# A sliding-window copy: some batches staged through SBUF beside a second ring of HBM-to-HBM copies

## The chip, the cores and the metric

The kernel runs on one core of a Trainium2 chip. The metric is the device time of one execution in microseconds. All runs here are of one core. The compute engines do next to nothing (0.2 us of 805.2 in the profile before): the program is DMA only, on the core's 16 DMA engines. Chips differ: on most of those used here the kernel before took 803 to 807 us, on one 818.8 us. Every kernel was therefore timed beside the kernel before on the same chip, and kernels from different chips are compared by that ratio.

## The reference

```python
batch, length, dim = (32, 4096, 256)       # x: float32, 134 MB
window_size, stride = 64, 32

n_windows = (length - window_size) // stride + 1      # 127
for i in range(n_windows):
    start = i * stride
    result[:, i] = x[:, start:start + window_size].copy()
```

Take 32 rows of 256 floats as one block: 32 KB. A batch has 128 blocks. Window i is block i followed by block i+1, 64 KB. So the output of a batch, 127 x 64 KB = 8.32 MB, is nearly twice its input of 4.19 MB. Each block except the first and the last goes to two places.

## The kernel before

It has several strategies. The one in use, `"d2d"`, copies windows straight from HBM to HBM on the one queue that the sync engine (SP) feeds. One DMA instruction copies 112 windows, a second one the remaining 15.

```python
STRATEGY = "d2d"
D2D_CHUNK = 112
D2D_NQ = 1

def _d2d_batch(q, x, out_flat, b, L, D, W, S, n_win):
    win_elems = W * D
    step_elems = S * D
    w0 = 0
    while w0 < n_win:
        nw = min(D2D_CHUNK, n_win - w0)
        src = bass.AP(x.tensor, x.offset + (b * L + w0 * S) * D,
                      [[step_elems, nw], [1, win_elems]])
        dst = out_flat[b * n_win + w0 : b * n_win + w0 + nw]
        q.dma_start(out=dst, in_=src, max_dma_last_dim=65536)
        w0 += nw

def _d2d(nc, x, out, B, L, D, W, S, n_win):
    out_flat = out.rearrange("b i w d -> (b i) (w d)")
    queues = [nc.sync, nc.scalar][:D2D_NQ]
    for b in range(B):
        _d2d_batch(queues[b % len(queues)], x, out_flat, b, L, D, W, S, n_win)
# ... (strategies "sbuf", "mix", "pair", "hybrid", which are not run)
```

Each window is one packet of 64 KB (4,064 in the trace, 32 x 127). Besides these, the trace has 992 small packets of 4 bytes, which is 32 x 16 + 32 x 15: as many as there are if every engine that takes part in a DMA posts one at its end, and if 112 windows run on 16 engines, seven each, and 15 windows on 15. I call them completion packets. From 739 us on, the shares of busy engines fit this too (0.94, or 15 of 16).

## Time and profile before

| | before |
|---|---|
| time | 807.23 us (806.14 to 807.51, 3 runs) |
| span of the profiled execution | 805.2 us |
| copied | 266.34 MB, so 266.34 MB read and 266.34 MB written |
| share of 16 engines' span with a packet | 98.3% |

These are lines of the profile page of the kernel before. The GB/s row has 40 equal slices of the span and counts each packet's bytes once. The queue's line gives packets, MB, and its packets' time as a share of 16 engines' span.

```profile
GB/s 313 355 322 332 342 316 352 322 339 335 319 358 313 322 352 319 348 329 335 339 316 358 319 329 348 313 361 319 335 335 332 342 322 339 332 322 332 326 335 254
q1 hardware_dynamic: 5056, 266.34, 98.3%
HBM read 266.34 MB, written 266.34 MB: 662 GB/s over the span
```

The engines always have a packet, but that does not say what limits the packets. The end of the run tells, because some engines run out of work there. This is the view by windows of time. Its columns are: window and its length, busy time of the one compute engine listed, clock, mean share of the 16 DMA engines that were busy, GB/s copied.

```profile
29.00:729.00 700.00, 0.00 (x0) 1.00 1.00 333
739.00:779.00 40.00, 0.00 (x0) 1.00 0.94 331
789.00:801.00 12.00, 0.00 (x0) 1.00 0.76 328
```

With 16, 15 and then 12 engines busy (shares 1.00, 0.94 and 0.76) the kernel copies 333, 331 and 328 GB/s. The packet records of the trace show the other side of it: a 64 KB packet takes 3.14 us on average with 16 engines busy and exactly 2.418 us with 12. An engine then does 65,536 B / 2.418 us = 27.1 GB/s, and at that rate 16 would do 434 (an estimate from the 2.418 us). Something that they share stops them at about 334 GB/s of copying, that is 668 GB/s of reads and writes.

### The profile page before, as it was taken

How to read it: one execution, taken by the hardware profiler on the slowest of the kernel's cores; microseconds unless marked ns; L12 is line 12 of the kernel's file. 1: busy time of each engine (PE TensorE's matmuls, PEld its weight loads, DVE VectorE, ACT ScalarE, POOL GpSimd, SP SyncE). 2: the span in 40 equal slices, each digit the busy share in tenths (PEclk: the TensorE clock that was granted, in tenths of full speed). 3: DMA queues.
4: the chain of work that ended last, by engine and by line, in shares of the span. 5: the costliest groups of instructions: out<-in, count | busy, mean ns of one | idle time of the engine just before them, and what ended most of it. 6: DMA issues, size and time to landing. Idle time of an engine off the chain costs nothing. (4 is left out here: it accounts for less than half of the span.)

```text
span 805.2 us, 109 instructions
## 1 busy us (share of the span) xinstructions
POOL 0.2 (0%) x4
## 2 busy tenths in 40 slices
POOL 0000000000000000000000000000000000000000
DMA  9999999999999999999999999999999999999995
GB/s 313 355 322 332 342 316 352 322 339 335 319 358 313 322 352 319 348 329 335 339 316 358 319 329 348 313 361 319 335 335 332 342 322 339 332 322 332 326 335 254
DMA packets 5056, 266.34 MB, mean 331 GB/s; under 512 B 992, under 2 KB 992, under 8 KB 992
## 3 DMA queue, kind: packets, MB, share of 16 engines
q1 hardware_dynamic: 5056, 266.34, 98.3%
HBM read 266.34 MB, written 266.34 MB: 662 GB/s over the span
## 5 line engine op out<-in xcount | busy, mean ns | idle before, releaser
L283 POOL MEMSET const-bfloat16-1.0<- 128x1 bf16 x1 | 0.1, 101 | 0.0
L283 POOL MEMSET const-uint8-127<- 128x1 uint8 x1 | 0.1, 101 | 0.0
L283 POOL MEMSET const-float32-0.0<- 128x1 f32 x1 | 0.1, 98 | 0.2 <-issue 0.2
L283 POOL MEMSET const-float32-1.0<- 128x1 f32 x1 | 0.1, 98 | 0.0
## 6 DMA issues: line engine op xcount, KB each, us to landing
out_dram<-in_x_dram SPq DMA_DIRECT2D x64, 100.5
```

The source lines that it names most:

```text
L283: nc = _bacc.Bacc("TRN2", target_bir_lowering=False, num_devices=1)
```

## The change

The intent: a batch that is staged in SBUF is read from HBM once instead of twice. Eight of the 32 batches (1, 5, ... 29) are loaded into SBUF tiles as [128 partitions x 32 KB] and stored twice, once as first halves of windows and once as second halves. The scalar engine (ACT) issues these on its own ring. The sync engine issues the other 24 batches as HBM-to-HBM copies on its ring, as before. To use 128 partitions, each store covers 128 half windows, one too many; the extra half lands in a window of a neighbouring batch, and that window is copied again after the store has landed. Windows that don't divide by 16 are cut otherwise: windows 113 to 125 of the 16 even batches go in one copy, meant to give each engine one batch, and other leftovers go in 4 KB pieces, 16 to a window. That each engine has one batch of that copy, and one piece of every window of the others, is an assumption.

The core of the diff, with cuts:

```diff
-STRATEGY = "d2d"
-def _d2d_batch(q, x, out_flat, b, L, D, W, S, n_win): ...
-# (all other strategies)
+class Copier:
+    def windows(self, q, b, w0, n):            # n windows of 64 KB
+        ... [[2 * blk, n], [1, 2 * blk]] <- [[blk, n], [1, 2 * blk]], max_dma_last_dim=65536
+    def windows_of(self, q, b0, step, n_b, w0, n):   # the same n windows of n_b batches
+        ...
+                out=self.oap((b0 * self.nw + w0) * 2 * blk,
+                    [[step * self.nw * 2 * blk, n_b], [2 * blk, n], [1, 2 * blk]]),
+                in_=self.xap(b0 * self.nb + w0,
+                    [[step * self.nb * blk, n_b], [blk, n], [1, 2 * blk]]),
+    def _shared(self, q, window, block, wstep, bstep, n, parts):   # 4 KB pieces, parts=16
+        e = 2 * blk // parts
+        ... [[e, parts], [wstep * 2 * blk, n], [1, e]] <- [[e, parts], [bstep * blk, n], [1, e]]
+    def load(self, q, t, b): ...      # 128 blocks of 32 KB -> 128 partitions
+    def store(self, q, t, b, half): ...
+class Staging: ...    # 4 tiles; semaphores loaded[i], stored[i]
...
+    with tc.tile_critical():
+        st.run(ring_s)
+
+        for b in sorted(evens + odds):
+            c.windows(ring_d, b, 1, 112)
+        c.windows_of(ring_d, 0, 2, 16, 113, last - 113)
+        for b in odds:
+            c.shared(ring_d, b, 113, n_win - 113)
+        c.shared_of(ring_d, odds[0], 4, len(odds), 0)
+        c.shared_of(ring_d, 0, 4, 8, 0)
+        c.shared_of(ring_d, 2, 4, 8, last)
+
+        for g in range(n_st - 1):
+            st.wait_stored(ring_d, g)
+        c.shared_of(ring_d, 0, 4, n_st - 1, last)
+        c.shared_of(ring_d, 2, 4, n_st - 1, 0)
+        st.wait_stored(ring_d, n_st - 1)
+        c.shared(ring_d, staged[-1] - 1, last, 1)
+        c.shared(ring_d, staged[-1] + 1, 0, 1)
+        ring_d.wait_ge(c.done, c.total)
```

More of the change, by code (lines that the diff above doesn't have):

```diff
@@ L4 @@
 import concourse.tile as tile
-from concourse import bass_utils, mybir
+from concourse import mybir
 from concourse._compat import with_exitstack
-STRATEGY = "d2d"
-NSB = 7
-D2D_CHUNK = 112
-def _d2d_batch(q, x, out_flat, b, L, D, W, S, n_win):
-    win_elems = W * D
-    step_elems = S * D
-    w0 = 0
-    while w0 < n_win:
-        nw = min(D2D_CHUNK, n_win - w0)
-        src = bass.AP(
-            x.tensor,
-            x.offset + (b * L + w0 * S) * D,
-            [[step_elems, nw], [1, win_elems]],
-        )
-        dst = out_flat[b * n_win + w0 : b * n_win + w0 + nw]
-        q.dma_start(out=dst, in_=src, max_dma_last_dim=65536)
-        w0 += nw
@@ L30 @@
-D2D_NQ = 1
-def _d2d(nc, x, out, B, L, D, W, S, n_win):
-    out_flat = out.rearrange("b i w d -> (b i) (w d)")
-    queues = [nc.sync, nc.scalar][:D2D_NQ]
-    for b in range(B):
-        _d2d_batch(queues[b % len(queues)], x, out_flat, b, L, D, W, S, n_win)
-class _SbufBatch:
-    def __init__(self, tc, ctx, x, out, B, L, D, W, S, n_win, bufs=3):
-        assert W % S == 0 and L % S == 0
-        self.m = W // S
-        self.n_blocks = L // S
-        assert self.n_blocks <= 128
-        self.blk = S * D
-        self.n_win = n_win
-        self.x_blocks = x.rearrange("b (n s) d -> b n (s d)", n=self.n_blocks)
-        self.out_rows = out.rearrange("b i w d -> b i (w d)")
-        self.pool = ctx.enter_context(tc.tile_pool(name="swin_sbuf", bufs=bufs))
-        self.dtype = x.dtype
-        self.chunks = []
-        w0 = 0
-        for cnt in (64, 48, 16, 15):
-            while n_win - w0 >= cnt or (w0 < n_win and cnt == 15):
-                cnt_eff = min(cnt, n_win - w0)
-                self.chunks.append((w0, cnt_eff))
-                w0 += cnt_eff
-        assert sum(c for _, c in self.chunks) == n_win
-    def alloc(self):
-        return self.pool.tile([self.n_blocks, self.blk], self.dtype, name="xb")
-    def load(self, q, t, b):
-        q.dma_start(out=t[:, :], in_=self.x_blocks[b])
-    def stores(self, q, t, b):
-        for k in range(self.m):
-            for (w0, cnt) in self.chunks:
-                src = t[w0 + k : w0 + k + cnt]
-                dst = self.out_rows[b, w0 : w0 + cnt, k * self.blk : (k + 1) * self.blk]
-                q.dma_start(out=dst, in_=src, max_dma_last_dim=65536)
@@ L76, in _sbuf @@
-def _sbuf(ctx, tc, nc, x, out, B, L, D, W, S, n_win):
-    sb = _SbufBatch(tc, ctx, x, out, B, L, D, W, S, n_win, bufs=4)
-    queues = [nc.sync, nc.scalar]
-    tiles = {}
-    for b in range(B):
-        t = sb.alloc()
-        tiles[b] = t
-        sb.load(queues[b % 2], t, b)
-        if b >= 1:
-            sb.stores(queues[(b - 1) % 2], tiles[b - 1], b - 1)
-            del tiles[b - 1]
-    sb.stores(queues[(B - 1) % 2], tiles[B - 1], B - 1)
-def _mix(ctx, tc, nc, x, out, B, L, D, W, S, n_win, nsb=None, lookahead=2):
-    if nsb is None:
-        nsb = NSB
-    out_flat = out.rearrange("b i w d -> (b i) (w d)")
-    sb = _SbufBatch(tc, ctx, x, out, B, L, D, W, S, n_win, bufs=4)
-    queues = [nc.sync, nc.scalar]
-    span = B - 4
-    sbuf_set = set()
-    if nsb > 0:
-        for j in range(nsb):
-            sbuf_set.add(1 + j * span // nsb)
-    assert len(sbuf_set) == nsb
-    def flush_stores(qidx):
-        t, bb = pending.pop(0)
-        j = 0
-        for (w0, cnt) in sb.chunks:
-            for k in range(sb.m):
-                q = queues[(qidx + j) % 2]
-                src = t[w0 + k : w0 + k + cnt]
-                dst = sb.out_rows[bb, w0 : w0 + cnt, k * sb.blk : (k + 1) * sb.blk]
-                q.dma_start(out=dst, in_=src, max_dma_last_dim=65536)
-                j += 1
-    pending = []
-    n_d2d_left = B - nsb
-    for b in range(B):
-        q = queues[b % 2]
-        if b in sbuf_set:
-            t = sb.alloc()
-            sb.load(q, t, b)
-            pending.append((t, b))
-            if len(pending) > lookahead:
-                flush_stores(b % 2)
-        else:
-            _d2d_batch(q, x, out_flat, b, L, D, W, S, n_win)
-            n_d2d_left -= 1
-            if pending and n_d2d_left < 2 * len(pending):
-                flush_stores(b % 2)
-    qi = 0
-    while pending:
-        flush_stores(qi)
-        qi += 1
@@ L136, in _pair @@
-def _pair(ctx, tc, nc, x, out, B, L, D, W, S, n_win, nsb=None):
-    if nsb is None:
-        nsb = NSB
-    assert 3 * nsb + 4 <= B - nsb, "not enough d2d batches to pair"
-    out_flat = out.rearrange("b i w d -> (b i) (w d)")
-    sb = _SbufBatch(tc, ctx, x, out, B, L, D, W, S, n_win, bufs=4)
-    queues = [nc.sync, nc.scalar]
-    blk = sb.blk
-    sbuf_batches = [4 * g for g in range(nsb)]
-    d2d_batches = [b for b in range(B) if b not in set(sbuf_batches)]
-    di = 0
-    W_CHUNKS = [(0, 64), (64, 48), (112, 15)]
-    L_CHUNKS = [(0, 64), (64, 48), (112, 16)]
-    def d2d_chunk(q, b, w0, cnt):
-        src = bass.AP(
-            x.tensor,
-            x.offset + (b * L + w0 * S) * D,
-            [[S * D, cnt], [1, W * D]],
-        )
-        q.dma_start(
-            out=out_flat[b * n_win + w0 : b * n_win + w0 + cnt],
-            in_=src,
-            max_dma_last_dim=65536,
-        )
-    def load_part(q, t, b, p0, cnt):
-        q.dma_start(out=t[p0 : p0 + cnt], in_=sb.x_blocks[b, p0 : p0 + cnt])
-    def store_part(q, t, b, w0, cnt, k):
-        src = t[w0 + k : w0 + k + cnt]
-        dst = sb.out_rows[b, w0 : w0 + cnt, k * blk : (k + 1) * blk]
-        q.dma_start(out=dst, in_=src, max_dma_last_dim=65536)
-    tiles = {}
-    n_groups = nsb + 2
-    for g in range(n_groups):
-        qa = queues[g % 2]
-        qb = queues[1 - g % 2]
-        a_instrs = []
-        if g < nsb:
-            bload = sbuf_batches[g]
-            t = sb.alloc()
-            tiles[bload] = t
-            for (p0, cnt) in L_CHUNKS:
-                a_instrs.append(("load", t, bload, p0, cnt, None))
-        if g >= 2:
-            bst = sbuf_batches[g - 2]
-            ts = tiles.pop(bst)
-            for (w0, cnt) in W_CHUNKS:
-                for k in range(sb.m):
-                    a_instrs.append(("store", ts, bst, w0, cnt, k))
-        b_needed = [ins[4] for ins in a_instrs]
-        b_instrs = []
-        nb_d2d = 3 if g < nsb else 2
-        for _ in range(nb_d2d):
-            bd = d2d_batches[di]
-            di += 1
-            for (w0, cnt) in W_CHUNKS:
-                b_instrs.append((bd, w0, cnt))
-        n = max(len(a_instrs), len(b_instrs))
-        for i in range(n):
-            if i < len(a_instrs):
-                ins = a_instrs[i]
-                if ins[0] == "load":
-                    load_part(qa, ins[1], ins[2], ins[3], ins[4])
-                else:
-                    store_part(qa, ins[1], ins[2], ins[3], ins[4], ins[5])
-            if i < len(b_instrs):
-                bd, w0, cnt = b_instrs[i]
-                d2d_chunk(qb, bd, w0, cnt)
-    rem = d2d_batches[di:]
-    for j, bd in enumerate(rem):
-        for (w0, cnt) in W_CHUNKS:
-            d2d_chunk(queues[j % 2], bd, w0, cnt)
@@ L215, in _hybrid, with __init__, xap, oap @@
-def _hybrid(ctx, tc, nc, x, out, B, L, D, W, S, n_win):
-    out_flat = out.rearrange("b i w d -> (b i) (w d)")
-    sb = _SbufBatch(tc, ctx, x, out, B, L, D, W, S, n_win, bufs=3)
-    sbuf_batches = [b for b in range(B) if (b + 1) * NSB // B > b * NSB // B]
-    d2d_batches = [b for b in range(B) if b not in set(sbuf_batches)]
-    q_d2d = nc.sync
-    q_sb = nc.scalar
-    pending = None
-    prefetch = None
-    for b in range(B):
-        if b in set(d2d_batches):
-            _d2d_batch(q_d2d, x, out_flat, b, L, D, W, S, n_win)
-        else:
-            t = sb.alloc()
-            sb.load(q_sb, t, b)
-            if pending is not None:
-                sb.stores(q_sb, pending[0], pending[1])
-            pending = (t, b)
-    if pending is not None:
-        sb.stores(q_sb, pending[0], pending[1])
+class Copier:
+    def __init__(self, nc, tc, x, out, B, L, D, W, S, n_win):
+        assert W == 2 * S and L % S == 0
+        self.nc, self.tc, self.x, self.out = nc, tc, x, out
+        self.B = B
+        self.blk = S * D
+        self.nb = L // S
+        self.nw = n_win
+        self.total = 0
+        self.done = tc.alloc_semaphore("done")
+    def xap(self, block, dims):
+        return bass.AP(self.x.tensor, self.x.offset + block * self.blk, dims)
+    def oap(self, elem, dims):
+        return bass.AP(self.out.tensor, self.out.offset + elem, dims)
+    def count(self, dma):
+        dma.then_inc(self.done, 16)
+        self.total += 16
+    def windows(self, q, b, w0, n):
+        blk = self.blk
+        self.count(
+            q.dma_start(
+                out=self.oap((b * self.nw + w0) * 2 * blk, [[2 * blk, n], [1, 2 * blk]]),
+                in_=self.xap(b * self.nb + w0, [[blk, n], [1, 2 * blk]]),
+                max_dma_last_dim=65536,
+            )
+        )
+    def windows_of(self, q, b0, step, n_b, w0, n):
+        blk = self.blk
+        self.count(
+            q.dma_start(
+                out=self.oap(
+                    (b0 * self.nw + w0) * 2 * blk,
+                    [[step * self.nw * 2 * blk, n_b], [2 * blk, n], [1, 2 * blk]],
+                ),
+                in_=self.xap(
+                    b0 * self.nb + w0,
+                    [[step * self.nb * blk, n_b], [blk, n], [1, 2 * blk]],
+                ),
+                max_dma_last_dim=65536,
+            )
+        )
+    def shared(self, q, b, w0, n, parts=16):
+        self._shared(q, b * self.nw + w0, b * self.nb + w0, 1, 1, n, parts)
+    def shared_of(self, q, b0, step, n_b, w, parts=16):
+        self._shared(
+            q, b0 * self.nw + w, b0 * self.nb + w, step * self.nw, step * self.nb, n_b, parts
+        )
+    def _shared(self, q, window, block, wstep, bstep, n, parts):
+        blk = self.blk
+        e = 2 * blk // parts
+        self.count(
+            q.dma_start(
+                out=self.oap(window * 2 * blk, [[e, parts], [wstep * 2 * blk, n], [1, e]]),
+                in_=self.xap(block, [[e, parts], [bstep * blk, n], [1, e]]),
+            )
+        )
+    def load(self, q, t, b):
+        return q.dma_start(
+            out=t[:, :], in_=self.xap(b * self.nb, [[self.blk, self.nb], [1, self.blk]])
+        )
+    def store(self, q, t, b, half):
+        blk = self.blk
+        w = b * self.nw - half
+        return q.dma_start(
+            out=self.oap(w * 2 * blk + half * blk, [[2 * blk, self.nb], [1, blk]]),
+            in_=t[:, :],
+        )
@@ new lines, with __init__, load, store @@
+class Staging:
+    def __init__(self, c, pool, dtype, batches, bufs):
+        self.c, self.batches = c, batches
+        self.tiles = [pool.tile([128, c.blk], dtype, name=f"xb{i}") for i in range(bufs)]
+        self.loaded = [c.tc.alloc_semaphore(f"loaded{i}") for i in range(bufs)]
+        self.stored = [c.tc.alloc_semaphore(f"stored{i}") for i in range(bufs)]
+    def load(self, q, g):
+        n, i = divmod(g, len(self.tiles))
+        if n:
+            q.wait_ge(self.stored[i], 32 * n)
+        self.c.load(q, self.tiles[i], self.batches[g]).then_inc(self.loaded[i], 16)
+    def store(self, q, g):
+        n, i = divmod(g, len(self.tiles))
+        q.wait_ge(self.loaded[i], 16 * (n + 1))
+        for half in (0, 1):
+            self.c.store(q, self.tiles[i], self.batches[g], half).then_inc(self.stored[i], 16)
+    def wait_stored(self, q, g):
+        n, i = divmod(g, len(self.tiles))
+        q.wait_ge(self.stored[i], 32 * (n + 1))
+    def run(self, q):
+        bufs = len(self.tiles)
+        for g in range(min(bufs, len(self.batches))):
+            self.load(q, g)
+        for g in range(len(self.batches)):
+            self.store(q, g)
+            if g >= 1 and g - 1 + bufs < len(self.batches):
+                self.load(q, g - 1 + bufs)
@@ L249 @@
     nc = tc.nc
-    W = int(window_size)
-    S = int(stride)
+    W, S = int(window_size), int(stride)
     B, L, D = x.shape
     n_win = (L - W) // S + 1
-    assert out.shape == (B, n_win, W, D), (out.shape, (B, n_win, W, D))
-    if STRATEGY == "d2d":
-        _d2d(nc, x, out, B, L, D, W, S, n_win)
-    elif STRATEGY == "sbuf":
-        _sbuf(ctx, tc, nc, x, out, B, L, D, W, S, n_win)
-    elif STRATEGY == "mix":
-        _mix(ctx, tc, nc, x, out, B, L, D, W, S, n_win)
-    elif STRATEGY == "pair":
-        _pair(ctx, tc, nc, x, out, B, L, D, W, S, n_win)
-    else:
-        _hybrid(ctx, tc, nc, x, out, B, L, D, W, S, n_win)
+    assert out.shape == (B, n_win, W, D)
+    c = Copier(nc, tc, x, out, B, L, D, W, S, n_win)
+    staged = list(range(1, B, 4))
+    evens = list(range(0, B, 2))
+    odds = list(range(3, B, 4))
+    n_st = len(staged)
+    last = n_win - 1
+    pool = ctx.enter_context(tc.tile_pool(name="xb", bufs=1))
+    st = Staging(c, pool, x.dtype, staged, 4)
+    ring_d, ring_s = nc.sync, nc.scalar
+    with tc.tile_critical():
[16 more added lines that the diff above has]
+        ring_d.wait_ge(c.done, c.total)
 _INS = ['x', 'window_size', 'stride']
```

## The prediction

> **What bounds the kernel now.** The page shows one DMA queue busy for 98.3% of 16 engines' span, and no compute. It copies 266.34 MB in 805.2 us, 331 GB/s; HBM carries reads and writes, 662 GB/s. Is the limit each engine's own rate, or something the engines share? The trace's packet records tell. With 16 engines busy, a 64 KB packet takes 3.13 us (20.9 GB/s an engine). From about 800 us only 12 engines have work, and each packet takes 2.418 us (27.1 GB/s), yet the total hardly falls: 334 GB/s with 16 busy, 330 with 15, 326 with 12. So they share about 334 GB/s of copying, 668 GB/s of HBM traffic. [...]
>
> I can't see here whether the shared limit counts reads and writes together. I assume so.
>
> **What the change does.**
> - Removes HBM reads. A staged batch is read once (4.19 MB) instead of twice (8.32 MB). Reads fall from 266.3 to 233.3 MB; writes are 266.9 MB (0.5 MB is overwritten). HBM traffic falls from 532.7 to 500.2 MB, 6.1%.
> - Adds engine bytes: a staged batch passes the engines as load and as stores. 199.8 + 100.7 = 300.4 MB instead of 266.3. At 434 GB/s that is 692 us, under the HBM time.
> - Evens the engines: 15-window chunks ran on 15 engines, so one had 224 packets, the others 256. Worth at most 2/256 of the time, 6 us, mostly hidden by the shared limit.
> - Adds 4 KB pieces: 152 an engine, about 10 MB, 30 us at the full rate; I estimate 10 us of loss, as nothing in this trace times such a copy.
> - Adds a serial tail: windows beside staged batches are rewritten once the staged stores land. Estimate 5 us.
> - Issue and semaphores: negligible. Before, issues ran about 100 us ahead of landing.
>
> All is on the critical path: the shared limit is busy from start to end.
>
> **Sum.** 500.2 MB / 668 GB/s = 749 us. Start and end as before, 5 us. With engines at 92% of their own rate both limits are near; 14 engines in the old tail gave 324, 3% under 334. Some of this and the 4 KB pieces: 12 us. **Predicted 766 us, 5% faster; 8 in 10 between 740 and 792.** Faster by over 2%: 0.87; within 2%: 0.09; slower: 0.04.
>
> **What the profile should show.**
> - HBM read about 233 MB, written about 267.
> - Two hardware queues at work together through most of the span, about 200 and 101 MB; total packet rate about 390 GB/s, HBM 645 to 665 GB/s.
> - 64 KB packets about 3 us or less; 32 KB packets 1.2 to 1.6 us.
> - If the rings take turns packet by packet, each engine has 192 staged packets against 181 large ones, so both end together, and the 4 KB pieces come last, at a lower rate in the last one or two slices.
>
> **What would make it wrong.** (1) The shared limit is on writes, 334 GB/s: no gain, about 800. (2) The rings do not overlap, because the long copy backlog holds up the staged ring: 199.8/334 + 100.7/434 = 830 us. (3) Staged packets or 8 MB-strided rows run slower in HBM. (4) Reads and writes mix better with staging, and the total passes 668: 735 or less.

The sum: 749 + 5 + 12 = 766 us. The 434 GB/s in it is 16 x 27.1, from the packets of 2.418 us. The 12 us are a guess beside the measured 324 GB/s of 14 engines; the 10 us for the 4 KB pieces and the 5 us for the tail in the list are guesses with no measurement behind them.

## The result, and the profile after

The changed kernel takes 786.01 us (785.48 to 787.29, 4 runs) against 807.35 us for the kernel before beside it. The ratio is 0.9739 with a 95% interval of 0.9726 to 0.9753: 2.6% faster. A ratio here is the mean time of one kernel's runs over that of the other's runs of the same rounds, so it is not quite the ratio of the medians. A later control on another chip (`after_again`) gave 0.9756.

The same lines of the profile page, now of the changed kernel; q1 is the sync engine's ring, q10 the scalar engine's.

```profile
GB/s 371 393 388 400 400 393 411 401 410 393 410 405 393 405 403 400 405 395 400 416 395 411 391 398 410 408 381 406 403 400 403 401 408 401 293 284 296 349 339 163
q1 hardware_dynamic: 5968, 199.76, 65.6%
q10 hardware_dynamic: 3456, 100.66, 33.3%
HBM read 233.31 MB, written 266.86 MB: 638 GB/s over the span
```

The bytes are those that were predicted. The row of slices has three parts: 34 slices near 400 GB/s (371 to 416), then three of 284 to 296, then an end that falls to 163. The window view of the same trace puts edges on them.

```profile
29.00:669.00 640.00, 0.00 (x0) 1.00 1.00 401
669.00:731.00 62.00, 0.00 (x0) 1.00 1.00 283
749.00:759.00 10.00, 0.00 (x0) 1.00 1.02 348
764.00:770.00 6.00, 0.00 (x0) 1.00 1.01 246
772.00:783.00 11.00, 0.00 (x0) 1.00 0.37 120
```

Read them from the top.

- **29 to 669 us: both rings at work.** The packet records split the 401 GB/s into 266 GB/s of HBM-to-HBM copies and 135.5 GB/s of staged packets. A copied byte costs HBM a read and a write, a staged packet only one of the two (2 x 199.76 + 100.66 = 500.2 MB, as the page has with 233.31 read and 266.86 written): 2 x 266 + 135.5 = 667 GB/s. Before it was 2 x 333 = 667. The shared limit is the same although the mix of reads and writes is not, so it counts the two together. I call it HBM's limit, because it fits HBM's traffic; which part on the way sets it is not shown.
- **669 to 731 us: 283 GB/s with every engine busy.** This is the copy of 13 windows of 16 batches (`windows_of`). Its 64 KB packets take 3.68 us instead of 2.60, and the staged 32 KB packets beside them 1.90 instead of 1.33.
- **749 to 759 us: the 4 KB pieces**, 348 GB/s. Nothing is lost here. The packet records give 692 GB/s of HBM traffic, 4% above 668: the shared limit is not quite the same for every pattern of access. The sum below takes it as fixed.
- **764 to 770 us: 246 GB/s with every engine busy.** These are still 4 KB pieces, so the end does not lose only by idle engines. The last 640 pieces, which begin about here (the 640th from the end starts at 766 us), come almost all from `shared_of`, where each engine, if it takes one of the 16 pieces of every window, steps four batches (16 MiB of source) from one piece to the next. Whether that step makes them slow was not tested.
- **772 to 783 us: only 37% of the engines are busy.** The engines don't finish together.

One sum holds all of it. In each stretch, take the HBM bytes that the packet records show (twice the copied, once the staged) and divide them by 668 GB/s; what the stretch took beyond that is its loss. The packets span 780.3 us, and 500.2 MB / 668 GB/s = 748.8 us.

| stretch, us from the span's start | loss before, us | | stretch | loss after, us |
|---|---|---|---|---|
| first packets, to 29 | 0.1 | | first packets, to 29 | 2.2 |
| 29 to 789 | 2.6 | | 29 to 669, both rings | 0.8 |
| | | | 669 to 731, copy of 16 x 13 windows | 17.8 |
| | | | 731 to 760, staged ring ends, 4 KB pieces | 1.9 |
| 789 to the end | 1.8 | | 760 to the end | 8.8 |
| sum | 4.5 | | sum | 31.5 |

So the reads that were saved are worth about 49 us (797 to 749), and some 27 us of that are given back, 18 of them in one copy instruction that moves 13.6 MB. The rest is about that copy and, less, about the end.

### The profile page after: what moved, and what is told of

The parts are those of the page before. It is cut to its first block, busy times and chain, and to the rows that moved or that the text cites. A ratio compares the mean times of both kernels' runs of the same rounds, so it can differ in the third digit from the quotient of the medians.

```text
span 783.8 us, 117 instructions
## 1 busy us (share of the span) xinstructions
POOL 0.2 (0%) x4
## 2 busy tenths in 40 slices
DMA packets 9424, 300.42 MB, mean 383 GB/s; under 512 B 1024, under 2 KB 1024, under 8 KB 3456
## 3 DMA queue, kind: packets, MB, share of 16 engines
q1 hardware_dynamic: 5968, 199.76, 65.6%
q10 hardware_dynamic: 3456, 100.66, 33.3%
HBM read 233.31 MB, written 266.86 MB: 638 GB/s over the span
```

## The experiments

The first theory for the slow copy: its source step from engine to engine is two batches, exactly 8 MiB (8,388,608 B, written as 8 MB from here on), and if all 16 engines walk through their batches at about the same pace, they read addresses 8 MB apart at the same time. That such reads slow each other down was a guess at this point. Rivals: the writes (15.9 MiB apart) are slow; one batch per engine is slow whatever the addresses; or it is slow because it stands at the end.

### Reads 32 KB and 4 KB off the 8 MB step

In `skew32k` each engine reads 32 KB earlier than it should, relative to its neighbour. Its output is wrong, which doesn't matter for the time. 195 of its 208 windows get other data; the first engine's stay; the number of packets and all writes stay the same.

```diff
-                    [[step * self.nb * blk, n_b], [blk, n], [1, 2 * blk]],
+                    [[step * self.nb * blk - blk, n_b], [blk, n], [1, 2 * blk]],
```

> Wrong result on purpose: in the one copy of 16 x 13 windows each engine reads 32 KB earlier than the engine before it would have it, so the 16 engines read 8 MB minus 32 KB apart instead of exactly 8 MB apart; every write stays as it is. Theory (the reads 8 MB apart collide in HBM): the stage of about 62 us loses its 18 us of excess, its 64 KB packets fall from 3.7 us to about 2.6 us, the kernel takes about 769 us. Rival (the writes, 15.9 MB apart, or one batch per engine, or the end of the rings is what is slow): 786 us, packets still 3.7 us.

`skew4k` is the same with 1024 elements (4 KB) in place of `blk`.

> The same wrong-result edit with 4 KB instead of 32 KB. [...] then also about 769 us. If the engines' reads need to be further apart than 4 KB, since each reads 64 KB in a row, something between 769 and 786.

Both ran on the slower chip (before: 818.76 us). `skew32k` took 781.52 us, ratio 0.9549 (0.9519 to 0.9578); `skew4k` 790.07 us, ratio 0.9652 (0.9622 to 0.9681); the unskewed kernel has 0.974 to 0.976 on two other chips (it was not run on this one). The window view of `skew32k`, both rings and then the stretch in which no engine has anything but the copy in question on its copying ring; on this chip that begins later:

```profile
29.00:669.00 640.00, 0.00 (x0) 1.00 1.00 393
689.00:725.00 36.00, 0.00 (x0) 1.00 1.00 374
```

And of `skew4k`:

```profile
29.00:669.00 640.00, 0.00 (x0) 1.00 1.00 394
688.00:731.00 43.00, 0.00 (x0) 1.00 1.00 329
```

This chip gives 393 to 394 where the others give 401. Measured against that, the copy runs at nearly the full rate with 32 KB (374; packets of 2.77 us), and about half way with 4 KB (329; 3.17 us; unskewed, it ran at 283 where the rings gave 401). The source addresses are the cause (why these are slow is not shown); the writes, the end of the program and one batch per engine are not, since all of these are unchanged. The expectation in absolute time (769 us) missed only because the chip was slower: 0.9549 of 807 us is 771 us. That 4 KB is enough did not hold here.

### The same copy in 13 parts, and at the start

`interleave` tries to cure it with the right result: 13 copies of one window of 16 batches, each after one of the copies of 112 windows.

```diff
-        for b in sorted(evens + odds):
-            c.windows(ring_d, b, 1, 112)
-        c.windows_of(ring_d, 0, 2, 16, 113, last - 113)
+        for j, b in enumerate(sorted(evens + odds)):
+            c.windows(ring_d, b, 1, 112)
+            if 6 <= j < 6 + last - 113:
+                c.windows_of(ring_d, 0, 2, 16, 113 + j - 6, 1)
```

> Right result. The copy of 16 x 13 windows is cut into 13 copies of 16 x 1 windows, one after each of 13 of the copies of 112 windows. Theory (it is 16 engines reading 8 MB apart at the same time): the engines stand up to 5 us apart in the middle of the run, so most of one engine's strided packets run beside other engines' ordinary ones, and most of the 18 us goes: 768 to 774 us. If each strided packet is slow by itself, wherever it stands: 786 us.

It took 788.56 us beside 818.76 us, ratio 0.9631 (0.9605 to 0.9658). Of the 0.019 that `skew32k` gains it gains about 0.011. The stretch that holds the parts runs at 388 GB/s, the stretches around it at 394. So spreading them out helps by half, less than the 768 to 774 us expected, which would be 0.951 to 0.959; each of them still costs something. (The engines stood 6 to 9 us apart in that part of the changed kernel, by the measure introduced below, and not up to 5.)

`strided_first` moves the line of the copy ahead of the loop.

> Right result. The copy of 16 x 13 windows is issued first instead of after the 24 copies of 112. Theory (8 MB apart): the loss moves to the start and stays 18 us: 784 to 788 us, 64 KB packets of 3.5 us or more in the first 65 us. Rival (it was slow because it ran at the end): 768 to 772 us.

Neither of the two: 807.79 us beside 818.76 us, ratio 0.9854 (0.9834 to 0.9874), 1.2% slower than the changed kernel by the ratios. In its trace the first 107 us run at 269 GB/s where 395 follow:

```profile
2.00:109.00 107.00, 0.00 (x0) 1.00 1.00 269
109.00:759.00 650.00, 0.00 (x0) 1.00 1.00 395
```

So the copy costs 107 x (1 - 269/395) = 34 us here and not 18. Its 64 KB packets take 5.5 us, the longest seen so far. "It was slow because it ran at the end" has fallen, but the theory lacked something.

### What the copy's cost depends on

The completion packets of one copy of 112 windows show how far apart the engines are: the time from the first engine's to the last one's. At the 24th copy, just ahead of the slow one, that was 12.2 us in the changed kernel and 14.9 us in its control, where the slow copy cost 15.1 us instead of 17.8. (The six runs whose program is the same up to there have 8.1 to 15.8 us.) The same 62 us in the control:

```profile
669.00:731.00 62.00, 0.00 (x0) 1.00 1.00 300
```

At the start there is hardly any: in the changed kernel the first 16 packets of the copying ring start within 0.6 us. The second theory: the reads collide when engines are at the same place in their batches at the same time, so the cost depends on how closely they keep in step. `resync` sets that alone, with the copy at its old place: the copying ring waits until its 24 copies have landed everywhere before it issues the slow one. `resync_skew` adds the 32 KB. Its output is wrong, which doesn't matter for the time.

```diff
+        ring_d.wait_ge(c.done, c.total)
         c.windows_of(ring_d, 0, 2, 16, 113, last - 113)
```

> Right result. The copying ring waits until its 24 copies of 112 windows have landed on all engines before it issues the copy of 16 x 13 windows, so the engines start that copy together instead of 12 us apart. Theory (the cost depends on how closely the engines keep in step: 18 us when they started 12 us apart, 35 to 37 us when together): the copy's packets take 5 us or more, it costs 30 us or more, and with the gap of the wait the ratio is 0.992 to 1.01. Rival (the spread doesn't matter, the other two kernels were slower for other reasons): only the gap, some 6 us, is added: 0.978 to 0.987.

> Wrong result on purpose: the same wait, and the reads 8 MB minus 32 KB apart. Both theories: no collision, packets of 2.6 to 2.8 us; only the gap of the wait is added to the kernel with these reads (0.955): 0.957 to 0.967. The difference between the two runs is the whole cost of the collision when the engines start together; theory 0.035 to 0.045, rival 0.018 to 0.025.

| on one chip (before 804.85 us) | time, us | ratio (95% interval) |
|---|---|---|
| resync | 799.33 | 0.9940 (0.9915 to 0.9964) |
| resync_skew | 768.50 | 0.9544 (0.9529 to 0.9559) |

The window view of `resync` within the slow copy:

```profile
689.00:749.00 60.00, 0.00 (x0) 1.00 1.00 235
```

And of `resync_skew`:

```profile
689.00:721.00 32.00, 0.00 (x0) 1.00 1.00 384
```

The two kernels differ in nothing but 32 KB of read address, and differ by 30.8 us. With engines that start together (the first packets of the copy start within 4 us) the collision costs 31 us, with engines 12 to 15 us apart 15 to 18 us. The wait changes the timing and leaves the addresses alone, so this bears the second theory out; the comparison with the second figure is across chips. The packets took 4.3 us on average, less than the 5 us that I had expected. The wait itself costs nothing visible, against the 6 us allowed for it: `resync_skew` has the same ratio as `skew32k` (0.9544 and 0.9549), as the staged ring fills the gap (423 GB/s in `resync_skew` from 669 to 679 us, with every engine busy).

### Do the rings have to overlap?

`serial_rings` lets the staged ring start only when the copies are done.

```diff
-        st.run(ring_s)
         ...
         for b in odds:
             c.shared(ring_d, b, 113, n_win - 113)
+        ring_s.wait_ge(c.done, c.total)
+        st.run(ring_s)
         ... (a second semaphore for the copies that follow)
```

> Right result. The staged ring starts only when the copies of the other ring are done, so the rings don't overlap. Theory (copying is held by HBM at 334 GB/s, staging by the engines at 434, and the gain is only in running both at once): 199.8/334 + 100.7/434 plus some 15 us: 840 to 855 us, ratio 1.04 to 1.06. If staging gains by itself: below 1.0.

It took 879.15 us beside 805.13 us, ratio 1.0922 (1.0900 to 1.0943). The bytes are the same as in the changed kernel. Windows of its trace, first the copies of 112 windows alone, then the copy of 16 x 13 windows alone, then the staged ring alone:

```profile
29.00:519.00 490.00, 0.00 (x0) 1.00 1.00 334
519.00:608.00 89.00, 0.00 (x0) 1.00 0.97 192
639.00:844.00 205.00, 0.00 (x0) 1.00 1.00 432
```

Alone, copies are held by HBM at 334 GB/s and staged packets by the engines at 432, each taking 1.21 us for 32 KB, an engine's 27 GB/s. Staging by itself is therefore a loss: HBM carries 432 of 668 GB/s, and by these rates a batch takes 12.58 MB / 432 GB/s = 29 us staged against 8.32 MB / 334 GB/s = 25 us copied (an estimate). The gain is only in running both at once, when HBM (667 of 668 GB/s) is filled and the engines (401 of 434) nearly so. The time came out above the 840 to 855 us expected because the slow copy costs 37 us here, for which that sum had no term (598 + 232 + 37 = 867 us; the rest is within the 15 us allowed): with one ring the engines kept in step here, 2.8 us apart at the copy before. This agrees with the second theory.

### Repairing the leftovers

A kernel with the right result has to do without the 8 MB step. `tail4k` copies those 208 windows in 4 KB pieces too, and issues four of the large copies in 32 KB packets so that both rings have about the same number of packets. (The 16 pieces of a window lie side by side. The new argument of `windows`, the packet size, is not shown in the cut below.) `after_again` is the changed kernel as a control.

```diff
         for b in sorted(evens + odds):
-            c.windows(ring_d, b, 1, 112)
-        c.windows_of(ring_d, 0, 2, 16, 113, last - 113)
-        for b in odds:
-            c.shared(ring_d, b, 113, n_win - 113)
+            c.windows(ring_d, b, 1, 112, 32768 if b % 8 == 2 else 65536)
+        for b in sorted(evens + odds):
+            c.shared(ring_d, b, 113, last - 113 + b % 2)
```

> The changed kernel unchanged, as a control, since chips differ: the last four runs were on a chip on which the kernel before took 818.8 instead of 807.4 us. Ratio to the kernel before 0.974 as recorded, whatever the chip; if it moves, ratios of different chips can't be compared closely.

> Right result, eight staged batches. The copy of 16 x 13 windows goes; those 208 windows are copied in 4 KB pieces like the other leftovers, and four of the 24 large copies run in 32 KB packets so that both rings have about the same number of packets (196 and 192 an engine). Theory (4 KB pieces run at the shared limit when alone, 342 GB/s in the changed kernel's trace; the 8 MB distance costs 18 us): ratio to before 0.949 to 0.956, 4 KB stage of about 72 us at 335 GB/s or more. Rival, the one of my prediction (4 KB pieces lose a third of their time): 0.975 or above.

`staged10` goes on from `tail4k` with batches 3 and 19 staged as well, and 12 of the 22 large copies in 32 KB packets.

```diff
-    staged = list(range(1, B, 4))
+    staged = sorted(list(range(1, B, 4)) + [3, 19])
     ... (packet sizes and leftovers to match)
```

> Right result, the same with ten staged batches and 12 of the 22 large copies in 32 KB packets. Theory (two limits: HBM 668 GB/s of reads and writes together, engines 434 GB/s): 492 MB of HBM traffic, part of it at the engines' limit: 744 us plus skew, ratio 0.930 to 0.943. If more staging gains nothing (the engines were the limit already): 0.95 or above.

In `left64` the leftovers go in 64 KB packets, 13 or 14 to a copy and so meant for as many engines (before, 15 windows ran on 15), right after the batch's large copy; `left64_10` is that with ten staged batches and nine of the 22 copied batches in 32 KB packets.

```diff
         for b in sorted(evens + odds):
             c.windows(ring_d, b, 1, 112)
-        c.windows_of(ring_d, 0, 2, 16, 113, last - 113)
-        for b in odds:
-            c.shared(ring_d, b, 113, n_win - 113)
+            c.windows(ring_d, b, 113, last - 113 + b % 2)
```

> Right result, eight staged batches. Neither the copy of 16 x 13 windows nor the 4 KB leftovers of 14 windows: after each copy of 112 windows the batch's next 13 or 14 windows follow in 64 KB packets, on 13 or 14 engines. Engines 13 to 15 then have 168 to 176 large packets, the others 192. Theory (the shared HBM limit evens the engines out while it binds; the busiest engine's 18.9 MB are 697 us at its own rate, below 749): ratio to before 0.936 to 0.953, that is 756 to 769 us at 807, so no worse than the kernel with all leftovers in 4 KB (0.953). If the uneven engines cost their full share (58 us on three engines): 0.965 or above.

> Right result, the same with ten staged batches and nine of 22 copied batches in 32 KB packets. Theory: HBM 492 MB / 668 = 736 us plus about 12 for skew and the last pieces, the busiest engine's 19.4 MB 716 us: ratio 0.925 to 0.943. If the engines' own rate binds already with ten: as the kernel with ten batches and 4 KB leftovers, 0.948, or worse.

| kernel | before beside it, us | time, us | ratio (95% interval) |
|---|---|---|---|
| after_again | 805.13 | 785.25 | 0.9756 (0.9742 to 0.9771) |
| tail4k | 805.13 | 767.38 | 0.9527 (0.9504 to 0.9551) |
| staged10 | 805.13 | 762.87 | 0.9478 (0.9462 to 0.9494) |
| left64 | 803.25 | 767.58 | 0.9544 (0.9521 to 0.9567) |
| left64_10 | 803.25 | 762.64 | 0.9485 (0.9462 to 0.9508) |

All are correct. Without the slow copy the kernel is 2.3% faster than the change, as the theory has it (`tail4k` also evens the rings' packets, so this figure is not the slow copy's alone), and the two with ten staged batches beat both kernels, 5.2% below the kernel before.

Windows of `tail4k`: both rings; 4 KB pieces alone; the last of them; the end.

```profile
29.00:649.00 620.00, 0.00 (x0) 1.00 1.00 408
709.00:744.00 35.00, 0.00 (x0) 1.00 0.99 326
746.00:758.00 12.00, 0.00 (x0) 1.00 1.00 214
758.00:766.00 8.00, 0.00 (x0) 1.00 0.36 125
```

The 4 KB pieces run at 326 GB/s, 2% below the limit, where I had expected 335. Then, with every engine busy, they fall to 214 for 12 us, which loses 4 us: again about where the `shared_of` copies with their steps of 16 MiB come. It is not the third of their time that the prediction allowed. `left64`, which has few of them, is no faster, and just misses the 0.936 to 0.953 expected:

```profile
750.00:766.00 16.00, 0.00 (x0) 1.00 0.33 133
```

Its end loses 8 us with a third of the engines busy and packets at or near an engine's full rate (2.4 us for 64 KB). Its shares are uneven by design (three engines have fewer large packets, if 13 windows run on 13), so this is not quite the loss at the end of the changed kernel. I found no repair for either.

The ten-batch kernels fell short of what I expected (0.930 to 0.943 and 0.925 to 0.943). The view of `staged10` shows why:

```profile
29.00:649.00 620.00, 0.00 (x0) 1.00 1.00 419
```

419 GB/s is 97% of the engines' 434, and the HBM traffic in this stretch is 406.9 MB / 620 us = 656 GB/s, 98% of 668. Both limits are near, and neither is filled quite. My estimate had taken each of them as filled in turn.

## Why the prediction was right or wrong

The prediction said 766 us, with 740 to 792 and faster by over 2% as likely. Measured: 786.0 us, 2.6% faster. The direction and the range held; the size was off by 20 us, so that the gain is half of what was forecast. The sum has 17 us on top of the 749; measured were 37: 17.8 in the slow copy, 8.8 at the end, 4.9 elsewhere, and some 5.5 outside the packets. That the miss is not larger is in part luck: 12 us allowed for losses that hardly came paid for part of one that was not counted.

- **"They share about 334 GB/s of copying, 668 GB/s of HBM traffic", counted as reads and writes together**: right. This was the assumption that the profile before could not show. The changed kernel's 640 us of 667 GB/s at another mix show it, and `serial_rings` shows each limit alone.
- **500.2 MB / 668 GB/s = 749 us**: right for the bytes (233.31 and 266.86 MB on the page), and right for the rate in the 640 us of both rings.
- **"Start and end as before, 5 us"**: too small. The kernel before took 807 us for bytes that need 797 at 668 GB/s, so about 10 us.
- **"The rings take turns packet by packet"**: right. In every 40 us between 80 and 680 us the records show about 160 packets of 64 KB and 160 of 32 KB. The counts are equal though the packets differ in size, which fits turns by packet, not by byte. The 32 KB packets took 1.33 us in the middle, within the 1.2 to 1.6 forecast.
- **"With engines at 92% of their own rate both limits are near", the 12 us that this and the 4 KB pieces share**: too pessimistic. The engines did run at 401 of 434 GB/s, but the whole stretch of 640 us lost 0.8 us, and most 4 KB pieces lost nothing (348 GB/s). Only the last ones did, 1.6 us at 764 to 770 us, with every engine busy.
- **The step that failed: the sum gives the copy of 16 x 13 windows the full rate.** "8 MB-strided rows run slower in HBM" stood only in the list of what could go wrong, with no size. It cost 17.8 us in the profiled run and 15.1 us in the control's; `skew32k` and `resync_skew` show that the step of the read addresses is what costs it, and `resync` that it costs 31 us when the engines are in step. The profile before has no such copy, so nothing measured gave a size for a term in the sum.
- **"Adds a serial tail ... estimate 5 us"**: the reason was wrong, and the 5 us stand in the list but not as a term of the sum. The waits for the staged stores cost nothing: the sync engine came to them at 757 us and passed the three that stand by themselves in 0.03 us each, as the staged ring had ended at 751 us. The end loses 8.8 us all the same. Of these, 2.0 us fall before 770 us, while nearly all engines are busy with slow 4 KB pieces, and 6.8 us after it, where the engines finish at different times. They drift apart while they alternate between two rings (from 5 us at the first copy to 12 us at the 24th; 1.4 to 2.8 us with one ring in `serial_rings`). That the drift is the cause of the uneven end is argued from the spread, not tested.

## What to carry to other kernels

When a copy is held by what the engines share and not by the engines (here 334 GB/s against 434), look for bytes that need not be read twice, and try that work on a second ring together with the copies. Here each alone left one of the two limits unfilled (copies 334 of the engines' 434 GB/s, staging 432 of HBM's 668), together they ran at 401 GB/s and 667 of HBM traffic, and one after the other they were slower than before (879 us against 805). Find out which of the two holds you from a place in the trace where some engines have run dry: here the total stayed (333, 331 and 328 GB/s with 16, 15 and 12 engines), so it was the shared one. And compute the distance between the addresses that the 16 engines read at the same time: 8 MiB there made a copy of 5% of the bytes give back a third of the whole gain (17.8 us), and with 32 KB less it ran at 384 GB/s instead of 235 on one chip (`resync_skew`, `resync`). Apart from 4 KB less (329 in `skew4k`), other distances were not tested by themselves.
